# Rows of the heads' scratch arrays in DRAM: 4352 bytes apart in place of 4104

## The chip, the cores and the metric

The kernel runs on one core of a Trainium2 chip. The metric is the device time of one execution in microseconds (us); shorter is better. The kernel before takes 1936.97 us (median of three runs, 1929.43 to 1939.34).

A core has engines that run side by side, each with its own list of instructions in a fixed order: TensorE (PE, matmuls; PEld is its loading of weights), VectorE (DVE), ScalarE (ACT), GpSimd (POOL) and SyncE (SP). An instruction waits for the semaphores of what it needs, and everything behind it on its engine waits with it. SP issues all of this kernel's transfers; 16 DMA engines carry them out, a row of a tile as one packet.

## The reference

One layer of a decoder trunk on 1024 tokens, of width 1024, with 16 learned tokens in front. Two branches of four heads each (GLA and mLSTM) read the same normed input, are gated and merged; a gated MLP with a causal convolution follows.

```python
def mixer_block(h, w_in, b_in, ...):
    proj = h @ w_in + b_in
    (g_q, g_k, g_v, g_r, g_lr, m_q, m_k, m_v, m_o, m_i, m_f, gate_a, gate_b) = jnp.split(proj, splits, axis=-1)
    ...
    o_gla = from_chunks(head_rms(o_gla, gla_norm)) * jax.nn.silu(g_r)
    ...
    o_ml = from_chunks(head_rms(o_ml, ml_norm)) * jax.nn.sigmoid(m_o)
    y = jax.nn.sigmoid(gate_a) * (o_gla @ w_branch_gla) + jax.nn.sigmoid(gate_b) * (o_ml @ w_branch_ml)
    return y @ w_out

def reference(...):
    h = h + mixer_block(rms_norm(h, norm_mix), ...)
    h = h + conv_ffn(rms_norm(h, norm_ffn), ...)
    return rms_norm(h, norm_final)[:, N_META:, :]
```

## The kernel before

Activations lie with channels on the 128 partitions and tokens along the row. Each float32 factor is split into a high and a low part (xH, xL and so on), and a product is the sum of three matmuls. After the input has been normed (xH, xL), the work goes in stages:

- **Gates and values** (to about 510 us). Gates g_r, m_o, gate_a and part of gate_b, and the values of the heads s = 2 to 7, are computed as 2 by 2 block products with seven multiplications; this holds for the values of heads s = 2 and 3 too, before and after the change alike. The gates go to DRAM: `rdr` (16 channel blocks), `gsc["a"]` and `gsc["b"]` (8 blocks each). `gate_store` writes each pair of blocks in two transfers, goA (the first 514 of a row's 1026 numbers) and goB (the other 512).
- **Heads** (about 510 to 1015 us). Eight heads, s = 0 to 3 by `gla`, s = 4 to 7 by `mlstm`. While one head's side chain runs (decay, scores, states, outputs on DVE, ACT and PE), PE fills the time with projections for the next head, and in the last two heads with the first GLA branch products (`branch_gla`, which reads the heads' outputs back into xH and xL by `load_og`, L1369). A table of numbers, FILL, fixes where the side chain's steps stand between the projections; the result is a fixed order per engine.
- **End of a head**, `post`: the head's output, 256 channels as two blocks j = 0, 1, is scaled (L591), transposed (L603), multiplied with the gate r (L605, L614), split into oH (L616) and the rest, left in r (L617), and stored to `osc[g, "H"]` (L618) and `osc[g, "L"]` (L619): four transfers of 128 rows of 1026 numbers per head. The buffers are few: oH of j = 0 shares its buffer (`of`) with KT of the next head (L800 in gla, L913 in mlstm), oH of j = 1 (`oH`) with An of the next head (L711), and the two r buffers are loaded anew by `load_r` (L507) for the next head. So each of these writes waits for the store that reads the buffer.
- **Loads in the heads' stage.** SP issues in its fixed order. Behind an r load that waits for a store stand the loads of weights (L102), of MB and WB (rows for mlstm, L873 and L875), of v (L498, L499) and of xH and xL.
- **Branches and output** (about 1015 to 1210 us). The rest of the GLA branch products, then the mLSTM branch products (L1453), which read `osc["m"]` back as omH and omL, the gates from `gsc` (yg, sb) and the finished products from `ysc`; then the product with w_out (L1832), whose sums go to `hsc` (rows of 1024 numbers).
- **MLP** (about 1210 us to the end).

The arrays that the change touches are osc (four of 8 blocks: g and m, H and L), gsc (two of 8), rdr (16) and ysc (8). A block is 128 rows, one for each partition, and a row has NP = 1026 float32 numbers, 4104 bytes. All transfers of these arrays move rows of 4104 bytes, or in `gate_store` of 2056 and 2048 bytes.

Of the kernel before, what the change touches and what calls it, by code (L numbers as in the profile page):

```python
# [9 lines left out]
F32 = mybir.dt.float32  # L10
# [7 lines left out]
P = 128  # L18
# [4 lines left out]
NK = D // P  # L23
NP = SEQ + 2
# [21 lines left out]
def hybrid_kernel(ctx, tc, x, meta, norm_mix, w_in, b_in, gla_w_gate, gla_b_gate, gla_norm,  # L46
# [17 lines left out]
    dram = ctx.enter_context(tc.tile_pool(name="dram", bufs=1, space=DRAM))  # L64
# [360 lines left out]
                                pattern=[[1, P]], channel_multiplier=-1)  # L425


    osc = {(g, p): dram.tile([NK, P, NP], F32, name=f"osc{g}{p}") for g in "gm" for p in "HL"}
    gsc = {g: dram.tile([NK, P, NP], F32, name=f"gsc{g}") for g in "ab"}
    rdr = dram.tile([2 * NK, P, NP], F32, name="rdr")  # L430
    rsc = dram.tile([2, H, T], F32, name="rsc")

    heads = {}
# [654 lines left out]
    def gate_piece(q, p):  # L1088

        n, at = (W0, W1)[p], W0 * p  # L1090
        V, X, Y, Z = (psG.tile([P, 512], F32, name=f"g{b}{q}_{p}", tag=f"{b}{p}") for b in "VXYZ")
        if p == 0:
            gout[q] = (gp.tile([P, 2, NA], F32, name=f"goA{q}", tag="oA", bufs=2),
                       gp.tile([P, 2, 512], F32, name=f"goB{q}", tag="oB"))
        oA, oB = gout[q]
        u2 = g_u2[:, p, :n]
        g1, g2 = (oA[:, i, at:at + n] for i in range(2))
        e1, e2 = (oB[:, i, 256 * p:256 * p + 256] for i in range(2))
        h2 = slice(n - 256, n)
        gate_product(V, q, p, "A12", "B21", True, True)  # L1100
        gate_product(X, q, p, "A11", "B11", True, True)
        with hp(PRI_E):
            nc.scalar.activation(g1, V[:, :n], AF.Copy)
            first.append(nc.vector.tensor_tensor(g1, X[:, :n], g1, OP.add))
        yield
        gate_product(Y, q, p, "S1", "T1", True, True)
        gate_product(Z, q, p, "S3", "T3", True, True)
        yield
        gate_product(X, q, p, "S2", "T2", False, True)
        with hp(PRI_E):  # L1110
            nc.scalar.activation(u2, X[:, :n], AF.Copy)
            nc.vector.tensor_tensor(e2, Y[:, h2], u2[:, h2], OP.add)
            nc.vector.tensor_tensor(e2, Z[:, h2], e2, OP.add)
        yield
        gate_product(Y, q, p, "S4", "B22", False, True)
        gate_product(Z, q, p, "A22", "T4", False, True)
        with hp(PRI_E):
            nc.vector.tensor_tensor(e1, Y[:, h2], u2[:, h2], OP.add)  # L1118
            nc.vector.tensor_tensor(g2, Z[:, :n], u2, OP.add)
        func, c = GP[q][3:]  # L1120
        for i, e, g in ((1, e2, g2), (0, e1, g1)):
            for v in (e, g):
                nc.scalar.activation(v, v, func, bias=cc(c + i))  # L1123
        yield
# [136 lines left out]
    for q in range(len(GP)):  # L1261
        for p in range(2):
            g = gate_piece(q, p)
# [95 lines left out]
        while not ready():  # L1359
            advance()  # L1360

    ysc = dram.tile([NK, P, NP], F32, name="ysc")
    og = []

    def load_og():
# [369 lines left out]
    def piece(q, p):  # L1735

        n = (W0, W1)[p]
        V, X, Y, Z = (psF.tile([P, 512], F32, name=f"{b}{q}_{p}", tag=f"{b}{p}") for b in "VXYZ")
        if q not in us:
            us[q] = [r2.tile([P, T], F32, name=f"ug{q}", tag="Y5"), r2.tile([P, T], F32, name=f"uu{q}", tag="Y2")] \  # L1740
                if q % 2 == 0 else [r2.tile([P, T], F32, name=f"u{i}{q}", tag=f"O{p_}3b") for i, p_ in enumerate("HL")]
            us[q].append(spare["u2"])
        ug, uu, u2 = us[q]
        u2 = u2[:, p, :n]
        g1, g2 = (u[:, W0 * p:W0 * p + n] for u in (ug, uu))
        e1, e2 = (u[:, 514 + 256 * p:770 + 256 * p] for u in (ug, uu))
        h2 = slice(n - 256, n)
        product(V, q, p, "A12", "B21", True, True)
        product(X, q, p, "A11", "B11", True, True)
        with hp(PRI_E):  # L1750
            nc.scalar.activation(g1, V[:, :n], AF.Copy)
            nc.vector.tensor_tensor(g1, X[:, :n], g1, OP.add)
        yield
        product(Y, q, p, "S1", "T1", True, True)
        product(Z, q, p, "S3", "T3", True, True)
        yield
        product(X, q, p, "S2", "T2", False, True)
        with hp(PRI_E):
            nc.scalar.activation(u2, X[:, :n], AF.Copy)  # L1759
            nc.vector.tensor_tensor(e2, Y[:, h2], u2[:, h2], OP.add)  # L1760
            nc.vector.tensor_tensor(e2, Z[:, h2], e2, OP.add)
        yield
        product(Y, q, p, "S4", "B22", False, True)
        product(Z, q, p, "A22", "T4", False, True)
        with hp(PRI_E):
            nc.vector.tensor_tensor(e1, Y[:, h2], u2[:, h2], OP.add)
            nc.vector.tensor_tensor(g2, Z[:, :n], u2, OP.add)
        yield
# [144 lines left out]
    for q in range(NJ):  # L1913
        for p in range(2):
            g = piece(q, 1 - p if q == NJ - 1 else p)
# [289 lines left out]
```

## Time and profile before

| | |
|---|---|
| median of three runs | 1936.97 us |
| the profiled execution's own time | 1939.23 us |
| its span | 1937.5 us |
| PE busy | 1863.5 us (96%) |
| DVE busy | 1297.9 us (67%) |
| ACT busy | 930.3 us (48%) |
| DMA, share of 16 engines' span | 57.8% |
| moved by DMA | 322.99 MB, mean 167 GB/s |

The profile is of one execution. Its slices are 40 equal parts of the span; a digit is the busy share in tenths. The timeline has one row for each instruction or run of like instructions: start and length in us, engine, line, operation, what is written and read, and in brackets the idle time before it and what ended it. SPq stands for SP's queue; its rows are the issues of transfers, not the transfers themselves. PEclk is the share of full clock that TensorE was granted.

### The profile page before, as it was taken

Reading aid. Unit: us, or ns where it says so; the run is one execution under the profiler, and the core shown is the slowest. Engines: PE = TensorE matmul, PEld = TensorE weight load, DVE = VectorE, ACT = ScalarE, POOL = GpSimd, SP = SyncE. Lnnn points to the kernel's source line nnn. Section 1 sums busy time; section 2 is a strip of 40 time slices with the busy share of each in tenths; the row PEclk is TensorE's granted clock in tenths of the full one; section 3 lists DMA queues with packets and bytes.
Section 4 is the critical chain, followed back from the end, with each engine's and each line's share of the span. In section 5 each row is a group of like instructions: output and inputs, shape, how many; then the busy total and the mean of one; then the engine's idle time right before and its main releaser. Section 6 shows DMA issues by size and latency. Waiting matters only on the chain. (4 is left out here: it accounts for less than half of the span.)

```text
span 1937.5 us, 32927 instructions
## 1 busy us (share of the span) xinstructions
PE 1863.5 (96%) x13221; PEld 1774.6 (92%) x13221; DVE 1297.9 (67%) x1965; ACT 930.3 (48%) x1595; POOL 242.8 (13%) x218
## 2 busy tenths in 40 slices
PE   8999999999999999898799999999999999999997
PEld 6999999999989998787798999999999999988886
DVE  7654555577566556665541566698878889877867
ACT  5344444433456678655430223854434344446645
POOL 4200000000122112000000000013222232200000
PEclk9999999999999999989899999999999999999999
DMA  4343444444504466589899988433333454689986
GB/s 147 91 120 110 126 112 118 124 146 137 159 22 110 99 88 110 116 144 221 205 152 276 306 314 318 137 112 112 100 115 104 147 162 142 188 270 334 363 292 223
DMA packets 256166, 322.99 MB, mean 167 GB/s; under 512 B 14439, under 2 KB 196961, under 8 KB 254349
## 3 DMA queue, kind: packets, MB, share of 16 engines
q1 hardware_dynamic: 256013, 320.88, 57.8%
q8 instruction: 104, 1.70, 0.4%
q14 instruction: 49, 0.40, 0.1%
HBM read 232.01 MB, written 88.82 MB: 166 GB/s over the span
## 5 line engine op out<-in xcount | busy, mean ns | idle before, releaser
L1966 DVE TENSOR_TENSOR ringL<-f,ringH 128x1024 fp32r<-128x1024 f32 (+1 forms) x76 | 79.9, 1066 | 19.3 <-ACT ringH L1965 19.2
L1965 ACT ACTIVATE ringH<-f 128x1024 fp32r<-128x1024 f32 (+1 forms) x76 | 69.2, 928 | 33.7 <-DMA f<-in_ffn_w_down_dram 25.8
L1832 PE MATMUL po<-wH_wo,yH 128*128 128x256 f32 x256 | 73.7, 288 | 0.7 <-DVE sb L1548 0.7
L1832 PE MATMUL po<-wL_wo,yH 128*128 128x256 f32 x256 | 73.7, 288 | 0.0
L1832 PE MATMUL po<-wH_wo,yL 128*128 128x256 f32 x256 | 73.3, 286 | 0.0
L681 POOL TENSOR_TENSOR pk<-pk,kT 128x256 f32<-128x256 f32 (+1 forms) x40 | 51.3, 1305 | 123.6 <-ACT pk L679 112.8
L1781 DVE SCALAR_TENSOR_TENSOR cv<-u,fc,cv 128x1024 f32<-128x1024 f32 x44 | 65.9, 1500 | 0.4
L1709 POOL TENSOR_TENSOR SB<-SA,rg 128x512 f32<-128x512 f32 x20 | 27.9, 1397 | 232.3 <-issue 100.7
L1691 POOL TENSOR_TENSOR A<-u2raw,A 128x512 fp32r<-128x512 f32 x20 | 43.3, 2164 | 87.8 <-ACT A L1690 87.8
L1066 POOL TENSOR_TENSOR gA<-gu2raw,gA 128x512 fp32r<-128x512 f32 x14 | 18.0, 1287 | 280.5 <-ACT gA L1065 280.5
L1690 ACT ACTIVATE HA<-rg 128x1024 fp32r<-128x1024 f32 x16 | 17.0, 1060 | 72.6 <-PE Y L1732 62.2
L1832 PEld LDWEIGHTS po<-wH_wo,yH 128*128 128x128 f32 x256 | 50.0, 195 | 0.9 <-issue 0.9
L2004 ACT ACTIVATE aH<-f 128x768 fp32r<-128x768 f32 (+1 forms) x38 | 35.5, 933 | 30.5 <-PE dV L2029 20.1
L1832 PEld LDWEIGHTS po<-wH_wo,yL 128*128 128x128 f32 x256 | 50.1, 196 | 0.0
L1832 PEld LDWEIGHTS po<-wL_wo,yH 128*128 128x128 f32 x256 | 50.0, 195 | 0.0
L2005 DVE TENSOR_TENSOR aL<-f,aH 128x768 fp32r<-128x768 f32 (+1 forms) x38 | 40.6, 1067 | 13.9 <-ACT aH L2004 12.0
L1383 PE MATMUL bg<-xL,wH_bg 128*128 128x342 f32 x120 | 39.9, 333 | 10.3 <-DMA xL<-oscgL 10.3
L1759 ACT ACTIVATE u2raw<-X 128x258 f32<-128x258 f32 (+1 forms) x44 | 16.4, 373 | 65.7 <-PE X L1732 65.7
L1453 PE MATMUL bm<-omL,wH_bm 128*128 128x342 f32 x144 | 46.1, 320 | 1.5 <-DMA omL<-oscmL 1.5
L1123 ACT ACTIVATE goB<-goB,col 128x256 f32<-128x256 f32 x56 | 28.2, 504 | 37.2 <-DVE goB L1118 22.3
L1453 PE MATMUL bm<-omH,wL_bm 128*128 128x342 f32 x144 | 46.0, 320 | 0.0
L1453 PE MATMUL bm<-omH,wH_bm 128*128 128x342 f32 x144 | 46.0, 319 | 0.0
(777 smaller groups left out, 7860.7 us busy)
## 6 DMA issues: line engine op xcount, KB each, us to landing
f<-wts SPq DMA_DIRECT2D x38, 512.0 KB
vr<-in_w_in_dram SPq DMA_DIRECT2D x24, 512.0 KB
wsH<-in_ffn_w_down_dram SPq DMA_DIRECT2D x11, 1024.0 KB
wts<-wsL SPq DMA_DIRECT2D x11, 1024.0 KB
rg<-in_ffn_w_up_dram SPq DMA_DIRECT2D x22, 512.0 KB
ru<-in_ffn_w_up_dram SPq DMA_DIRECT2D x22, 512.0 KB
ad<-a SPq DMA_DIRECT2D x44, 256.0 KB
wr_wo<-in_w_out_dram SPq DMA_DIRECT2D x18, 512.0 KB
```

Source lines behind the costliest of these rows:

```text
L681: nc.gpsimd.tensor_tensor(e, e, k, OP.mult)
L1123: nc.scalar.activation(v, v, func, bias=cc(c + i))
L1383: nc.tensor.matmul(pts[i][:, :n], a[:, k, :], b[k][:, t0:t0 + n], start=(k == 0 and m == 0), stop=(k == NK - 1 and m == 2))
L1453: nc.tensor.matmul(pts[i][:, :n], a[:, k, :], b[k][:, t0:t0 + n], start=(k == 0 and j == 0), stop=(k == NK - 1 and j == 2))
L1691: eng.tensor_tensor(l, src, h.bitcast(F32), OP.subtract)
L1709: late.tensor_tensor(sb[:, 0:4], sa[:, 0:4], rg[:, 0:4], OP.subtract)
L1781: nc.vector.scalar_tensor_tensor(y, u[:, j:SEQ + j], fc[:, j, jj:jj + 1], y, OP.mult, OP.add)
L1832: nc.tensor.matmul(pt[:, :DV], a, b[:, k % 4, :], start=(k == 0 and i == 0), stop=(k == NK - 1 and i == len(terms) - 1))
L1965: nc.scalar.activation(h, raw, AF.Copy)
L1966: splits.append(nc.vector.tensor_tensor(l, raw, h.bitcast(F32), OP.subtract))
L2004: nc.scalar.activation(h, a[:, :n], AF.Copy)
L2005: nc.vector.tensor_tensor(l, a[:, :n], h.bitcast(F32), OP.subtract)
```

## The change

The four osc arrays, the two gsc arrays, rdr and ysc are allocated with rows of 1088 numbers (4352 bytes), and every use goes through a view of the first 1026 numbers of each row. The 62 numbers behind are neither written nor read. What is computed, the transfers, their sizes in bytes and the order of the instructions on each engine stay as they are. The distance between a head's H and L arrays goes from 1024 rows of 4104 bytes to 1024 rows of 4352 bytes.

```diff
-    osc = {(g, p): dram.tile([NK, P, NP], F32, name=f"osc{g}{p}") for g in "gm" for p in "HL"}
-    gsc = {g: dram.tile([NK, P, NP], F32, name=f"gsc{g}") for g in "ab"}
-    rdr = dram.tile([2 * NK, P, NP], F32, name="rdr")
+    osc = {(g, p): dram.tile([NK, P, 1088], F32, name=f"osc{g}{p}")[:, :, :NP] for g in "gm" for p in "HL"}
+    gsc = {g: dram.tile([NK, P, 1088], F32, name=f"gsc{g}")[:, :, :NP] for g in "ab"}
+    rdr = dram.tile([2 * NK, P, 1088], F32, name="rdr")[:, :, :NP]
...
-    ysc = dram.tile([NK, P, NP], F32, name="ysc")
+    ysc = dram.tile([NK, P, 1088], F32, name="ysc")[:, :, :NP]
```

## The prediction

> **What bounds the kernel now.** I read the page first, and in it the slices, since a mean over the span hides stages.
>
> ```profile
> PE   8999999999999999898799999999999999999997
> DMA  4343444444504466589899988433333454689986
> GB/s 147 91 120 110 126 112 118 124 146 137 159 22 110 99 88 110 116 144 221 205 152 276 306 314 318 137 112 112 100 115 104 147 162 142 188 270 334 363 292 223
> ```
>
> A slice is 48.4 us. TensorE is the bound nearly everywhere, so a change pays only where PE falls below 9: slices 16, 18 and 19 (775 to 823 us and 872 to 969 us), the stage of the heads. There the DMA row and the GB/s row disagree: slice 20 has its engines 9 tenths busy for 152 GB/s, slice 37 as busy for 363 GB/s. Something in the heads' stage makes transfers long without moving bytes. So I asked for windows around single transfers (columns: the stretch, its length, busy time of five engines, granted clock, DMA share, GB/s; a packet counts whole in the window where it starts, so a share can pass 1):
>
> ```profile
> 603.00:604.50 1.50, 1.50 (x11) 1.50 (x10) 1.50 (x4) 0.00 (x0) 0.00 (x0) 1.00 0.98 380
> 604.50:611.00 6.50, 6.50 (x47) 6.48 (x46) 6.25 (x9) 3.94 (x5) 2.87 (x2) 1.00 0.73 68
> 686.00:704.00 18.00, 18.00 (x130) 17.23 (x129) 9.99 (x11) 16.99 (x30) 3.98 (x5) 1.00 0.98 93
> 912.00:930.00 18.00, 9.53 (x40) 6.99 (x38) 11.05 (x18) 7.31 (x13) 0.00 (x0) 0.90 1.18 89
> 118.50:120.50 2.00, 2.00 (x19) 2.00 (x18) 1.44 (x4) 1.73 (x3) 0.00 (x0) 1.00 0.96 345
> 953.00:954.50 1.50, 1.50 (x12) 1.50 (x11) 1.20 (x5) 0.00 (x0) 0.12 (x1) 1.00 0.82 331
> 1198.00:1201.00 3.00, 3.00 (x27) 3.00 (x27) 0.93 (x3) 1.02 (x4) 0.00 (x0) 1.00 0.99 362
> 938.00:942.00 4.00, 4.00 (x17) 3.60 (x17) 0.71 (x4) 1.31 (x5) 0.00 (x0) 0.75 1.03 417
> ```
>
> The stores of the window at 1198 are SP's row
>
> ```profile
> 1197.46 1.19 SPq L1617 DMA_DIRECT2D hsc<-h  x2
> ```
>
> At 603 us the first of a head's four stores into osc (513 KB, 128 rows of 4104 bytes end to end) runs at 380 GB/s. When the second follows at once, the rate falls to 68 GB/s and stays there until both are drained; four in a row hold the queue near 90 GB/s for 18 us (686 and 912). Three controls stand below. At 118.5 us goA is stored into the same kind of array, rows 4104 bytes apart but only 2056 bytes of each: 345 GB/s. At 953 us ysc, whole rows, one store alone: 331 GB/s. At 1198 us two stores of hsc back to back, rows of 4096 bytes, 4096 apart: 362 GB/s for 3 us. And loads of 4104-byte rows run at 417 GB/s (938). So neither volume nor reading is slow; whole 4104-byte rows, laid end to end and written one store after another, are.
>
> What waits for them, in order of time (engine rows of the timeline; in brackets the idle time before the row and what ended it):
>
> ```profile
> 762.73 0.60 ACT L711 ACTIVATE An<-sct 128x512 f32<-128x512 f32 x1 [3.70 <-DMA oscgH<-oH]
> 824.37 1.29 DVE L913 TENSOR_TENSOR KT<-kt,tcol 128x512 f32<-128x512 f32 x2 [6.43 <-DMA oscgH<-oH]
> 848.64 0.20 DVE L897 COPY gp<-WB 128x8 f32<-128x8 f32 x1 [4.13 <-DMA WB<-rsc]
> 896.23 0.17 DVE L897 COPY gp<-WB 128x8 f32<-128x8 f32 x1 [3.93 <-DMA WB<-rsc]
> 917.94 1.29 DVE L913 TENSOR_TENSOR KT<-kt,tcol 128x512 f32<-128x512 f32 x2 [5.04 <-DMA oscmH<-oH]
> 1039.75 1.23 DVE L1497 TENSOR_TENSOR yg<-bg,yg 128x1026 f32<-128x1026 f32 x1 [22.75 <-DMA yg<-gsca]
> ```
>
> An and KT are written into the buffers that oH was stored from, so they wait until the store has read them. WB waits differently: SP issues in order, and its load of r ahead of WB waits for the store of the old r.
>
> ```profile
> SPq L507 <- DMA oscgL<-r: 103.4, 8, 16.4
> 908.01 0.32 SPq L618 DMA_DIRECT2D oscmH<-oH  x1
> 909.69 0.32 SPq L619 DMA_DIRECT2D oscmL<-r  x1
> 910.91 0.32 SPq L618 DMA_DIRECT2D oscmH<-oH  x1
> 912.17 0.32 SPq L619 DMA_DIRECT2D oscmL<-r  x1
> 912.54 0.45 SPq L1369 DMA_DIRECT2D xL<-oscgL  x1
> ```
>
> The first row is SP's wait list: 103.4 us in 8 times. The others are its issues: a load of xL right behind four stores. What reaches TensorE:
>
> ```profile
> 772.38 0.27 PE L790 MATMUL k0t<-ident,kh 128*16 128x128 f32 x1 [3.06 <-DVE kh L770]
> 805.55 0.33 PE L603 MATMUL ot<-ident,or 128*128 128x128 f32 x1 [1.89 <-ACT or L591]
> 825.12 2.08 PE L920 MATMUL msc<-qc,kc 128*128 128x128 f32 x8 [5.85 <-DVE KT L913]
> 855.64 0.33 PE L603 MATMUL ot<-ident,or 128*128 128x128 f32 x1 [1.19 <-ACT or L591]
> 900.41 1.53 PE L603 MATMUL ot<-ident,or 128*128 128x128 f32 x4 [3.11 <-ACT or L591]
> 918.69 0.70 PE L937 MATMUL u<-v,K 16*128 16x257 f32 x2 [3.63 <-DVE KT L913]
> 935.46 0.65 PE L1383 MATMUL bg<-xL,wH_bg 128*128 128x342 f32 x1 [10.29 <-DMA xL<-oscgL]
> 1041.12 0.39 PE L1453 MATMUL bg<-xH,wH_bg 128*128 128x342 f32 x1 [2.88 <-DVE yg L1497]
> 1055.82 0.43 PE L1453 MATMUL bm<-omL,wH_bm 128*128 128x342 f32 x1 [1.48 <-DMA omL<-oscmL]
> ```
>
> After such a gap the granted clock is 0.50 for a while (columns as above):
>
> ```profile
> 772.80:776.20 3.40, 3.40 (x16) 3.40 (x15) 3.34 (x3) 2.23 (x6) 0.00 (x0) 0.50 1.06 310
> 825.20:834.20 9.00, 9.00 (x24) 7.02 (x25) 5.58 (x10) 3.95 (x8) 0.00 (x0) 0.50 1.13 67
> 902.50:905.90 3.40, 3.40 (x15) 2.99 (x14) 1.26 (x3) 2.96 (x7) 0.00 (x0) 0.50 0.63 251
> 919.60:923.00 3.40, 3.40 (x9) 2.66 (x9) 3.40 (x5) 1.79 (x5) 0.00 (x0) 0.50 1.22 75
> 935.50:940.00 4.50, 4.50 (x14) 4.14 (x15) 0.16 (x1) 0.38 (x1) 0.00 (x0) 0.50 1.00 406
> 1042.50:1045.80 3.30, 3.30 (x13) 3.30 (x12) 2.36 (x2) 0.00 (x0) 0.00 (x0) 0.50 0.99 397
> ```
>
> **The change, part by part.** It adds and removes no instruction and moves none: the order on all five engines is the same, and every transfer keeps its 4104 (or 2056 and 2048) bytes per row. Only addresses change: a row begins 4352 bytes after the last, 17 times 256, so every row starts at a multiple of 256 from its array's start, and 248 unwritten bytes part it from the next.
>
> The unknown is the rate of whole-row stores at the new pitch, one behind another. Bounds by the nearest rows: 362 GB/s (hsc, separate aligned starts) and 93 GB/s (now); and below nothing, if lone row ends cost more than shared ones (a rival below). I take the fast end, since the new stores resemble the hsc pair in start and the goA store in not touching their neighbours, and both ran fast. A store of 525,312 bytes then takes 1.4 us at 362 to 380 GB/s.
>
> The loads of these rows gain nothing: 417 GB/s already. The stores of gsc, rdr and ysc gain nothing either where they come singly (345 and 331). So everything hangs on osc: eight heads with four stores each. Early heads (602 to 740 us) have their slow drains under a busy PE, so they gain nothing. From 760 us on, gap by gap:
>
> 772: ACT's 3.70 us on An goes; kh follows on ACT and DVE. 3.70 is more than PE's 3.06, so **3.1**. 825: DVE was ready for KT at 817.94 (824.37 less 6.43) and KT takes 1.29, so it ends at 819.2; PE arrives at 819.27 (825.12 less 5.85). The whole **5.9** goes. 918: likewise KT at 912.90 to 914.2, PE there at 915.06: **3.6**. 855 and 900: these chains run through gp, whose waits of 4.13 and 3.93 exceed PE's 1.19 and 3.11: **4.3**. 935: four stores and the load behind them are five transfers of 1.4 us, 7 us from 908.8, so xL lands near 917 even with 1 us for the issue; PE wants it at 925.17, or about 5 us earlier once 918 is mended, 920: **10.3**. 1041 and 1055: yg waits 22.75 us behind the last head's stores and stores of ysc; with those drained PE's 2.88 and 1.48 go: **4.4**. Sum of gaps: 31.6.
>
> Clock: the six stretches at 0.50 hold 3.4 + 9.0 + 3.4 + 3.4 + 4.5 + 3.3 = 27.0 us of matmuls; at full clock they take half: **13.5**. The 1.89 at 805 has no store wait in front and stays. Together 45.1 us.
>
> What is late next: with gaps closed, PE meets the ends of the heads' scalar chains sooner, as at 805, where 1.89 us cost another 3.4 us at half clock, 1.7 in loss. I leave two such places, 3.6 us each: 7 us given back. So 38 us from the profiled execution's own 1939.2 (span 1937.5 and 1.7 around it): **1901 us**. That execution lies 2.3 above the median of 1936.97 and at the slow end of three that differ by 9.9 us; I count from its own rows.
>
> **Against the trace: two rules.** The 417 GB/s of loads whose rows start at any multiple of 8 bytes is the row for the first. The Trainium skill, DMA: Bandwidth & Descriptors, section How a descriptor splits into AXI transactions, says that a read which does not start on 256 bytes fetches from the boundary below; for 4104 bytes I work out an estimate of 137 beats against 129, 6%. By that alone the sum would be zero, as the transfers that wait here are not 6% but four times too long. The rows at 686 and 912, four times below 362, are the ones for the second: the same page, section Latency and other measured facts, reports that padding a 4 MiB row pitch by 192 bytes left copies slow, and by 4 KiB made them fast. Its pitches are far larger than ours, yet it speaks against 248 bytes as a cure; by it the sum is again zero. The hsc pair, at a pitch of 4096 and fast, shows that a round pitch near this size is no harm here.
>
> **The rivals.** *Half a cure*: what costs is an incomplete line at a row's end. Today both ends of nearly every row are incomplete, later only the last 8 bytes. For it: hsc, without any, is fast. Against: goA has as many and is fast. A store's drain would halve: 18 us of drain become 9. The KT wait at 825 would end near 819, the xL load near 922; most gaps close, but WB, yg and a few us at 935 stay. I give it half to two thirds of 38, 19 to 25: about 1917.
>
> *No cure*: the slowness comes from the two arrays (H and L lie 1024 rows, 4.0 MiB now and 4.25 MiB later, apart) or from stores in a row as such. For it: the single stores at 603 and 953 are fast, and the slow ones are always H and L mixed. Against: the hsc pair. It gives the time of now, 1937. The two rules above belong here, with this chance.
>
> *Slower*: now the end of one row and the start of the next fall into one line and may be completed together; with a gap, 128 lone ends per store never are. Place: the drain behind L618 and L619. If a store took half as long again as now, 18 us becoming 27, KT in four heads (6.43, 5.04 and two smaller) would wait some 4 us more each and xL 9 more, less what the gaps before it already shift: about 20 us, 1957. It decides once four stores take longer than the 18 us of now. Against it: goA, whose row ends are lone when it is stored, at 345 GB/s.
>
> **How the numbers follow.** Full cure 0.70 (1890 to 1911: 45 us and a little of 805 at the best, 28 at the worst), half 0.13 (1911 to 1925), none 0.11 (1932 to 1941), slower 0.06 (1950 to 1965). The range 1890 to 1925 takes in the first two, 0.83, less a little at their edges. A measurement of this kernel tells about 0.5%, 9.7 us, from no change, so faster is under 1927: 0.70 + 0.13 = 0.83; same 0.11; slower 0.06.
>
> **What would show it.** Right: four osc stores drained within 7 us of the first, at over 300 GB/s; KT, An and gp without DMA waits; L507 on SP waiting for oscL a few us in place of 103.4; PE without the gap at 935, and clock 0.50 only near 772 or 805. The slices 17 to 20 should show lower DMA shares. Wrong: drains of 90 GB/s again (no cure), of some 180 (half), or gaps of the same length that now wait for DVE or ACT chains in place of DMA, which would mean that I missed what is late next.

## The result and the profile after

| | before | after |
|---|---|---|
| median | 1938.15 us (4 runs, 1929.43 to 1943.69) | 1885.66 us (4 runs, 1882.99 to 1888.39) |
| ratio | | 0.9733 (95%: 0.9693 to 0.9773) |
| profiled execution, own time | 1939.23 us | 1884.03 us |
| its span | 1937.5 us | 1882.3 us |
| PE busy | 1863.5 us (96%) | 1846.2 us (98%) |
| packets of the kernel's DMA queue (q1), share of 16 engines' span | 57.8% | 51.8% |

Faster, by 52.5 us between the medians and 55.2 between the profiled executions. The forecast was 1901 (1890 to 1925): the sign and the mechanism hold, and the gain is larger than the range allowed.

The slices of the page of after, each 47.1 us:

```profile
PE   7999999999999999999999999999999999999997
DMA  4334344345513143247758987433333545589986
GB/s 151 92 115 116 111 126 114 122 146 157 170 29 104 54 135 104 92 163 278 263 207 297 316 304 275 131 100 109 108 100 113 162 141 165 180 307 330 369 279 226
```

PE is at 9 in every slice but the first and the last. Counted from 0, as in the prediction, slice 17 (800 to 847 us) now has its DMA engines 4 tenths busy for 163 GB/s and slice 18 7 tenths for 278; before, slice 17 had them 8 tenths busy for 144 and slice 18 9 tenths for 221.

Windows around the stores into osc in after (columns as in the prediction):

```profile
602.50:604.00 1.50, 1.50 (x13) 1.48 (x12) 1.50 (x5) 0.91 (x1) 0.00 (x0) 1.00 0.98 386
673.50:681.00 7.50, 7.50 (x57) 7.50 (x55) 7.50 (x11) 4.16 (x5) 1.42 (x2) 1.00 0.82 305
886.00:892.00 6.00, 6.00 (x43) 5.33 (x42) 5.22 (x11) 1.14 (x2) 0.00 (x0) 1.00 1.03 372
```

The first store runs as before (386 against 380 GB/s). Four in a row, which were held near 90 GB/s, now move at 305 to 372. SP's timeline shows the same from the side of who waits. The rows are those of head 1, first of before, then of after; a load of r (L507) can only start once the store that reads its buffer (L619) has ended:

```profile
672.06 0.33 SPq L618 DMA_DIRECT2D oscgH<-oH  x1
...
686.83 0.32 SPq L507 DMA_DIRECT2D r<-rdr  x1
702.03 0.32 SPq L507 DMA_DIRECT2D r<-rdr  x1
```

```profile
673.01 0.33 SPq L618 DMA_DIRECT2D oscgH<-oH  x1
674.27 0.33 SPq L619 DMA_DIRECT2D oscgL<-r  x1
676.69 0.32 SPq L618 DMA_DIRECT2D oscgH<-oH  x1
678.00 0.32 SPq L619 DMA_DIRECT2D oscgL<-r  x1
678.42 0.40 SPq L507 DMA_DIRECT2D r<-rdr  x1
682.09 0.53 SPq L507 DMA_DIRECT2D r<-rdr  x1
```

From the head's first store to the second load of r it was 30.0 us; it is 9.1. SP's wait list of after says it for all heads:

```profile
SPq L507 <- DMA oscgL<-r: 18.6, 6, 6.2
SPq L507 <- DMA oscmL<-r: 5.9, 3, 2.3
```

Together these are 24.5 us; before, the two kinds took 103.4 and 31.9.

The DMA row does not show the whole of such a drain. In head 0 of before, L was stored at 603.36 and the load of r that waits for this store was issued at 616.49, yet in the last 4 us no packet starts (columns as above):

```profile
612.50:616.40 3.90, 3.90 (x27) 3.90 (x26) 3.90 (x5) 2.08 (x3) 3.29 (x3) 1.00 0.00 0
```

In after the two issues stand at 601.88 and 605.25. When a store has ended is therefore read from who waits for it. What DVE waits for on DMA between 755 and 1060 us, before and then after (us in total, times, longest):

```profile
DVE yg L1497 <- DMA yg<-gsca: 23.4, 2, 22.8
DVE KT L913 <- DMA oscmH<-oH: 10.2, 3, 5.0
DVE gp L897 <- DMA WB<-rsc: 9.0, 3, 4.1
DVE KT L913 <- DMA oscgH<-oH: 6.4, 1, 6.4
```

```profile
DVE wsL L1525 <- DMA wsp<-wspL: 7.5, 1, 7.5
```

All four are gone. What is left of PE's waits between 755 and 1250 us in after (every entry over 0.3 us):

```profile
PE ot L603 <- ACT or L591: 1.9, 1, 1.9
PE sct L710 <- DVE A L734: 1.6, 1, 1.6
PE htp L1643 <- ACT hn L1628: 1.6, 2, 0.8
PE Y L1732 <- DVE uu L1760: 1.1, 1, 1.1
PE htp L1643 <- ACT hT L1649: 0.8, 1, 0.8
PE po L1832 <- DVE sb L1548: 0.7, 1, 0.7
PE bg L1453 <- DVE bs L1387: 0.6, 1, 0.6
PE k0t L790 <- DVE kh L770: 0.4, 1, 0.4
```

No DMA is among them, and neither KT nor xL. The 1.9 is the wait that stood at 805 and now stands at 801. Stage by stage (the same stretches of before, then of after):

```profile
805.00:855.00 50.00, 43.05 (x220) 37.88 (x220) 29.74 (x73) 29.29 (x56) 2.11 (x5) 0.83 0.91 144
900.00:950.00 50.00, 35.45 (x175) 30.29 (x176) 21.59 (x40) 20.53 (x45) 0.00 (x0) 0.83 0.93 217
```

```profile
805.00:855.00 50.00, 50.00 (x311) 45.98 (x311) 38.03 (x81) 35.70 (x65) 2.11 (x4) 1.00 0.55 189
900.00:950.00 50.00, 50.00 (x302) 46.42 (x301) 29.96 (x70) 22.66 (x54) 1.79 (x1) 1.00 0.63 235
```

In 50 us PE now runs 302 to 311 matmuls where it ran 175 to 220. It has no gap there and a granted clock of 1.00 instead of 0.83.

### The profile page after: what moved, and what is told of

Same layout as the page of the kernel before. It is cut to its first block, busy times and chain, and to the rows that moved or that the text cites. A ratio compares the mean times of both kernels' runs of the same rounds, so it can differ in the third digit from the quotient of the medians.

```text
span 1882.3 us, 32927 instructions
## 1 busy us (share of the span) xinstructions
PE 1846.2 (98%) x13221; PEld 1760.5 (94%) x13221; DVE 1298.1 (69%) x1965; ACT 930.2 (49%) x1595; POOL 241.5 (13%) x218
## 3 DMA queue, kind: packets, MB, share of 16 engines
q1 hardware_dynamic: 256013, 320.88, 51.8%
## 4 chain that ended last, share of the span: by engine, by line
PE 82%; DVE 7%; ACT 4%; DMA 2%; issue 2%; POOL 1%; SPq 0%; DVEq 0%; POOLq 0%; ACTq 0%
PE pj L172 9%; PE Y L1732 6%; PE Z L1732 6%; PE X L1732 6%; PE bm L1453 5%; PE gX L1083 4%; PE gY L1083 4%; PE gZ L1083 3%; PE V L1732 3%; PE bg L1383 3%; PE po L1832 3%; PE dY L2029 2%; PE dZ L2029 2%; PE dX L2029 2%; PE pv L217 2%
## 5 line engine op out<-in xcount | busy, mean ns | idle before, releaser
L1690 ACT ACTIVATE HA<-rg 128x1024 fp32r<-128x1024 f32 x16 | 17.0, 1060 | 72.6 <-PE Y L1732 72.6
L2004 ACT ACTIVATE aH<-f 128x768 fp32r<-128x768 f32 (+1 forms) x38 | 35.5, 933 | 32.4 <-PE dV L2029 22.3
L1123 ACT ACTIVATE goB<-goB,col 128x256 f32<-128x256 f32 x56 | 28.2, 503 | 37.2 <-DVE goB L1118 22.3
L1118 DVE TENSOR_TENSOR goB<-gY,gu2raw 128x256 f32<-128x256 f32 x28 | 11.8, 421 | 49.5 <-PE gY L1083 49.5
```

## The experiments

All kernels keep the computation, the transfers and the order of instructions; only the addresses of scratch arrays differ. The arrays are allocated one behind another in the order of the program (gH, gL, mH, mL for osc), so one array's size is the distance between a head's H and L block. Sizes were set and addresses were not seen, so all distances below rest on this order. Each group ran on one chip beside the kernel before, whose median was 1933.04 (13 runs), 1932.82 (7) and 1934.14 (16).

### Which arrays

**osc_only** changes osc alone:

```diff
-    osc = {(g, p): dram.tile([NK, P, NP], F32, ...) for g in "gm" for p in "HL"}
+    osc = {(g, p): dram.tile([NK, P, 1088], F32, ...)[:, :, :NP] for g in "gm" for p in "HL"}
```

> Only the four osc arrays get rows 4352 bytes apart; gsc, rdr and ysc stay at 4104. If all of the gain comes from the heads' stores into osc (theory), the time is that of the changed kernel, 1886 us within 4. If the single stores of gsc, rdr and ysc count as well (rival), 5 to 15 us of the 52 are missing: 1891 to 1901.

**others_only** changes gsc, rdr and ysc, and leaves osc:

```diff
-    gsc = {g: dram.tile([NK, P, NP], F32, ...) for g in "ab"}
-    rdr = dram.tile([2 * NK, P, NP], F32, ...)
+    gsc = {g: dram.tile([NK, P, 1088], F32, ...)[:, :, :NP] for g in "ab"}
+    rdr = dram.tile([2 * NK, P, 1088], F32, ...)[:, :, :NP]
...
-    ysc = dram.tile([NK, P, NP], F32, ...)
+    ysc = dram.tile([NK, P, 1088], F32, ...)[:, :, :NP]
```

> gsc, rdr and ysc get rows 4352 bytes apart; osc stays at 4104. Theory (osc alone): the time of before, 1938 us within 5. Rival (the others count): 1923 to 1933.

osc_only took 1884.61 us, ratio 0.9745 (0.9730 to 0.9761); others_only 1932.95, ratio 0.9996 (0.9981 to 1.0011). PE's wait list of others_only still begins

```profile
PE bg L1383 <- DMA xL<-oscgL: 11.0, 1, 11.0
PE u L937 <- DVE KT L913: 6.0, 2, 5.3
PE msc L920 <- DVE KT L913: 6.0, 2, 4.1
PE ot L603 <- ACT or L591: 6.0, 2, 4.0
```

So the whole gain comes from osc, and padding the three other arrays does nothing for the time; the 1938 that was expected for it was an earlier median of before. In osc_only PE waits for yg no more, though gsc, from which yg is loaded, and ysc are as before: that load stood behind the osc stores. DVE still waits 12.8 us for yg there, where it waited 22.8; in after it does not. One thing in others_only is not explained: its two early heads drain in 8.9 and 22.3 us where before takes 13.1 and 30.0 (measured as in the table below), although osc is the same. With one trace of each kernel, differences of this size in the drains are not to be relied on, and no time came of them.

### Which heads

**osc_g** pads only the arrays of heads 0 to 3, **osc_m** only those of heads 4 to 7:

```diff
-    osc = {(g, p): dram.tile([NK, P, NP], F32, ...) for g in "gm" for p in "HL"}
+    osc = {(g, p): dram.tile([NK, P, 1088 if g == "g" else NP], F32, ...)[:, :, :NP] for g in "gm" for p in "HL"}
```

> Only the osc arrays of heads 0 to 3 get rows 4352 bytes apart. If the gain is the sum of the waits that I listed, each by the store it hangs on, this takes away 772 (3.1 and 1.7 of clock), 825 (5.9 and 4.5) and 855 (1.2): 16 us, so 1917 beside 1933 for before. Rival: the gaps hang together, and a gap closed early is paid again at the next slow store: under 8 us, over 1925.

(osc_m has `g == "m"` in that place.)

> Only the osc arrays of heads 4 to 7 get rows 4352 bytes apart. By the sum of waits it takes away 868 (0.6), 900 (3.1 and 1.7), 918 (3.6 and 1.7), 935 (10.3 and 2.3), 1041 and 1055 (4.4 and 1.7), and what lay behind 1060 us in the profile of before (the first product of the second norm, 3.1 of its 3.9 us, and its clock, about 2): 34 us, so 1899 beside 1933. With osc_g it should add up to the 48 of all four within 5. Rival: the two add up to less than 40 or more than 56.

osc_g took 1909.21 us, ratio 0.9890 (0.9864 to 0.9916), 23.6 less than before; osc_m 1903.58, ratio 0.9853 (0.9825 to 0.9882), 29.2 less. Together 52.8 against 48 for both halves at once: within the scatter, the two add up. The waits left on PE are those of the half that is not padded; osc_g first, osc_m second:

```profile
PE u L937 <- DVE KT L913: 5.2, 1, 5.2
PE bg L1383 <- DMA xL<-oscgL: 4.0, 1, 4.0
PE bm L1453 <- DMA omL<-oscmL: 3.0, 1, 3.0
```

```profile
PE msc L920 <- DVE KT L913: 6.0, 1, 6.0
PE ot L603 <- ACT or L591: 5.8, 2, 3.9
PE k0t L790 <- DVE kh L770: 3.1, 1, 3.1
```

The split differs from what was expected by 5 to 8 us each way. The load of xL at 935 reads a padded array in osc_g and PE still waits 4.0 us for it; in osc_m, where it is not padded, PE does not wait. What holds it are the stores of the mLSTM heads ahead of it in SP's queue. In osc_g this wait fell by 6.3 us, most of what osc_g gained beyond its forecast. The forecast of osc_m had counted some 5 us behind 1060 us that were not the stores' (see the base of the prediction below); without them it is 29 us, beside 29.2 measured.

### The gap between rows, the start of rows, or the distance of the arrays

The change alters three things at once: rows no longer touch, they start at multiples of 256 bytes, and the H and L arrays move apart, from 4 MiB + 8 KiB to 4 MiB + 256 KiB. The following eight take them apart. The old line of osc is the same in each diff and is left out.

**far_apart**: rows end to end as before, blocks and arrays as far apart as in the change.

```diff
+    osc = {(g, p): dram.tile([NK, P * 1088], F32, ...)[:, :P * NP].rearrange("k (p n) -> k p n", n=NP) for g in "gm" for p in "HL"}
```

> osc keeps rows end to end, 4104 bytes apart, but each block of 128 rows starts where it does in the changed kernel, so H and L lie the same 4.25 MiB apart as there. If the slowness comes from the distance of the two arrays (rival), 1886 us. If it comes from the rows themselves, their starts or their touching ends (theory), 1938 us within 5 and drains of four stores near 90 GB/s.

**pitch4360**: a gap of 256 bytes, but rows that start at multiples of 8 bytes only.

```diff
+    osc = {(g, p): dram.tile([NK, P, 1090], F32, ...)[:, :, :NP] for g in "gm" for p in "HL"}
```

> osc rows 4360 bytes apart: a gap of 256 bytes between rows as in the changed kernel, but rows start at any multiple of 8 bytes, as before. If touching row ends cost (theory A), 1886 us within 4. If starts off a boundary cost (theory B), 1938 us within 8, since 7 of 8 rows start off every 64-byte boundary.

pitch4360 took 1885.45 us, ratio 0.9749 (0.9731 to 0.9766): the whole gain, so aligned starts are not needed. far_apart was expected at the time of before and took 1895.75, ratio 0.9814 (0.9791 to 0.9837): most of the gain with rows that touch. The theory that touching rows alone are at fault fell here, and the rival that was called *No cure* in the prediction, the distance between the arrays, came back.

**arrays_apart**: rows and blocks end to end, only the arrays as far apart as in the change.

```diff
+    osc = {(g, p): dram.tile([NK * P * 1088], F32, ...)[:NK * P * NP].rearrange("(k p n) -> k p n", p=P, n=NP) for g in "gm" for p in "HL"}
```

> osc rows end to end, 4104 bytes apart, blocks of 128 rows end to end as before (525,312 bytes), but the arrays H and L as far apart as in the changed kernel (4.25 MiB in place of 4 MiB and 8 KiB). far_apart had both distances and gained 37 of 48 us. If the distance of H and L is what counts, 1896 us; if the distance of block 0 and block 1 is, 1933; if both count in part, between them.

**pitch4112**: a gap of 8 bytes.

```diff
+    osc = {(g, p): dram.tile([NK, P, 1028], F32, ...)[:, :, :NP] for g in "gm" for p in "HL"}
```

> osc rows 4112 bytes apart: 8 bytes between rows, so most rows still share a stretch of 64 bytes with the next; blocks lie 526,336 bytes and H and L 4 MiB and 16 KiB apart, near the distances of before. If rows in one stretch of 64 bytes cost, or the near distances do, 1925 to 1938; if only ends that meet byte to byte cost, 1885 within 5.

arrays_apart took 1902.25 us, ratio 0.9849 (0.9826 to 0.9873); pitch4112 1893.16, ratio 0.9801 (0.9769 to 0.9832). pitch4112 lies 8 us above what was expected of a gap alone. Its gap of 8 bytes brings 40 us, but it also moves the arrays to 4 MiB + 16 KiB apart. Four more separate the two:

**apart8**: end to end, the arrays 8 MiB + 8 KiB apart. **apart16k** is the same line with 1028 * 1024 numbers, 4 MiB + 16 KiB apart.

```diff
+    osc = {(g, p): dram.tile([2099200], F32, ...)[:NK * P * NP].rearrange("(k p n) -> k p n", p=P, n=NP) for g in "gm" for p in "HL"}
```

> osc rows end to end as before; each array takes 8 MiB and 8 KiB, so that H and L lie 8 KiB past a multiple of 4 MiB apart, as before, but are no longer neighbours. If the distance by its remainder is what arrays_apart changed (theory D), 1933 us within 5. If any larger distance helps (rival), 1895 to 1907.

> osc rows end to end, arrays 4 MiB and 16 KiB each: the distance of H and L of pitch4112 without its 8 bytes between rows. If the gap made pitch4112's 40 us (theory A), 1925 to 1937; if its 8 KiB of distance did (theory D), 1890 to 1905.

**padded_apart8**: rows 4352 bytes apart as in the change, the arrays 8 MiB + 8 KiB apart.

```diff
+    osc = {(g, p): dram.tile([2099200], F32, ...)[:NK * P * 1088].rearrange("(k p n) -> k p n", p=P, n=1088)[:, :, :NP] for g in "gm" for p in "HL"}
```

> osc rows 4352 bytes apart, arrays of 8 MiB and 8 KiB. If the gap between rows is enough by itself (theory A), 1885 us within 4, whatever the distance. If the distance by its remainder counts beside it (theory D), 1895 to 1925.

**pitch4160**: a gap of 56 bytes, rows that start at multiples of 64.

```diff
+    osc = {(g, p): dram.tile([NK, P, 1040], F32, ...)[:, :, :NP] for g in "gm" for p in "HL"}
```

> osc rows 4160 bytes apart: every row starts on 64 bytes and none shares 64 bytes with the next; H and L 4 MiB and 64 KiB apart. If a shared stretch of 64 bytes is what pitch4112 (1893) had left, 1885 us within 4; if it is the distance, 1890 to 1897.

All of them together. "Head 0" is the time from the issue of its first L store to the load of r behind it, "head 1" from its first store to the second load of r (the two stretches shown for before and after above), both from SP's timeline of the profiled execution.

| | gap, bytes | H to L beyond a multiple of 4 MiB | median us | ratio (95%) | head 0, us | head 1, us |
|---|---|---|---|---|---|---|
| before | 0 | 8 KiB | 1932.8 to 1934.1 | | 13.1 | 30.0 |
| apart8 | 0 | 8 KiB | 1930.74 | 0.9986 (0.9956 to 1.0016) | 13.0 | 27.9 |
| apart16k | 0 | 16 KiB | 1919.42 | 0.9918 (0.9889 to 0.9947) | 12.0 | 28.5 |
| arrays_apart | 0 | 256 KiB | 1902.25 | 0.9849 (0.9826 to 0.9873) | 7.4 | 16.9 |
| far_apart | 0 (blocks apart) | 256 KiB | 1895.75 | 0.9814 (0.9791 to 0.9837) | 7.3 | 11.8 |
| pitch4112 | 8 | 16 KiB | 1893.16 | 0.9801 (0.9769 to 0.9832) | 3.4 | 9.1 |
| pitch4160 | 56 | 64 KiB | 1886.76 | 0.9752 (0.9716 to 0.9787) | 3.4 | 9.1 |
| padded_apart8 | 248 | 8 KiB | 1888.86 | 0.9754 (0.9712 to 0.9797) | 3.1 | 9.1 |
| pitch4360 | 256 | 264 KiB | 1885.45 | 0.9749 (0.9731 to 0.9766) | 2.9 | 9.1 |
| after | 248 | 256 KiB | 1885.66 | 0.9733 (0.9693 to 0.9773) | 3.4 | 9.1 |

What lies behind the last column: the same 10 us of head 1, from 3 us after its first store, in apart8, arrays_apart, far_apart, pitch4112 and after:

```profile
676.50:686.50 10.00, 10.00 (x72) 10.00 (x72) 10.00 (x14) 5.45 (x6) 2.47 (x3) 1.00 1.15 80
676.80:686.80 10.00, 10.00 (x73) 10.00 (x71) 10.00 (x14) 5.45 (x6) 2.49 (x3) 1.00 1.16 128
676.00:686.00 10.00, 10.00 (x73) 10.00 (x72) 10.00 (x15) 5.45 (x6) 2.33 (x3) 1.00 1.03 225
678.00:688.00 10.00, 10.00 (x73) 10.00 (x72) 10.00 (x14) 5.44 (x6) 2.52 (x3) 1.00 0.84 264
676.00:686.00 10.00, 10.00 (x72) 10.00 (x71) 10.00 (x14) 5.46 (x6) 2.48 (x3) 1.00 0.80 261
```

With rows that touch the queue moves 80 GB/s at the old remainder of 8 KiB, 128 with the arrays 256 KiB past 4 MiB apart, and 225 with the blocks apart as well; with a gap of 8 or 248 bytes it moves 264 or 261. Three readings follow.

First, with touching rows the distance decides. Its size does not: at 8 MiB + 8 KiB (apart8) nothing is gained that is clear of the scatter, at 4 MiB + 256 KiB 31 us (arrays_apart). far_apart, with the blocks apart too, gains 37 us; the intervals of the two just overlap, so the distance between blocks probably counts as well. Second, with a gap the distance no longer matters much: padded_apart8 gains 45.3 us at the old remainder and osc_only 48.4 at 256 KiB, while padded_apart8 and apart8, at the same distance, differ by 42 us (1930.74 to 1888.86). Third, 8 bytes are most of the gap's worth: apart16k and pitch4112 have the same distance between H and L and differ by 26 us, each counted from its own chip's before as 14.7 and 39.7 us gained, 25 between them. So apart16k fits neither of its two forecasts; the gap and the 8 KiB of distance share pitch4112's 40 us. In these runs slow drains need both, rows that touch and an unlucky distance, and the change removed both; the gap alone would have brought 45 us (1934.14 to 1888.86), the distance alone 31 to 37.

osc_only, pitch4360, pitch4160 and the change itself lie within 2.2 us of each other; no version was found that is faster than the change.

## Why the prediction was right in its mechanism, and where it failed

**The mechanism held**, point by point. Four osc stores drain at 305 to 372 GB/s, as was taken from hsc and goA. An, KT and gp wait for no DMA. L507's waits fell from 103.4 to 18.6 us for oscgL; the 10.29 at 935 is gone; the only gap behind 750 us that still costs clock in the heads' stage is the one that stood at 805. That gsc, rdr and ysc gain nothing was right (others_only, 0.9996).

**Gaps and clock: 45.1 us in the sum, 48.2 measured.** The gaps of the sum, 31.6 us, shrink to 0.4 (k0t). A way to check the sum without trusting single rows is to compare the start of the same group in both kernels. The mLSTM branch products, first and last start in us at the end of the times (their ns are shortest, median and longest), before and then after:

```profile
L1453 PE MATMUL bm<-omH,wH_bm x144: 313/319/328, 1054.0 to 1145.4; 128*128 128x342 f32 x144
```

```profile
L1453 PE MATMUL bm<-omH,wH_bm x144: 315/319/328, 1008.9 to 1098.2; 128*128 128x342 f32 x144
```

After leads by 45.1 at the first and by 47.2 at the last. That the first equals the sum is chance: 1.48 us of the sum fall between the two, at 1055, and before the first of the gaps after was not level but 0.95 behind (head 1's first store, 672.06 and 673.01 above). So this stretch gained 48.2, 3.1 more than the sum. Two waits that the sum had left out are 1.7 of it: PE waits for S at 785 (1.3 us before, 0.2 after) and for KT at 868 (0.6 before, none after). The rest was not traced to single rows.

**What is late next: the first step that failed.** It took 7 us off for two new places like 805, 3.6 each. There is none: the waits of PE on the heads' DVE and ACT chains that the list above still has stood there before too, the 1.9 at 805 and 1.5 us where after has 1.6 (sct). The prediction gave these chains a price without a row that showed one being late. That they had slack hidden behind the DMA waits would explain it; the slack was not measured. Counting 45.1 from 1939.23 gives 1894, within the range.

**The base: the second step that failed.** The prediction counted from the profiled execution's own 1939.2, "from its own rows". The three groups of experiments gave before medians of 1932.8 to 1934.1 in 36 runs, 5.1 to 6.4 us lower. Take off the 7 us, the 3.1 and these 5.1 to 6.4, and 1901 becomes 1884.5 to 1885.8, beside the 1885.66 measured. The fast end of the range, 1890, allowed 45 us and a little of 805 from the high base, and neither a longer sum nor a lower base.

**The rest, to 55.2, does not come from the osc stores.** After's lead grows by 8 us more behind 1146, where no osc store is near. Of these, 5.3 are one place in before: the transposes htp that start at 1226.44 in before start at 1173.89 in after, a lead of 52.5. PE's wait list of before (755 to 1250 us) has

```profile
PE htp L1643 <- ACT hn L1628: 3.9, 1, 3.9
```

The timeline of DVE has the work ahead of it, and a window the clock behind it:

```profile
1205.22 1.23 DVE L1525 TENSOR_TENSOR wsL<-wsH 128x1024 f32<-128x1024 f32 x1 [3.33 <-DMA wsH<-in_ffn_w_down_dram]
```

```profile
1211.20:1216.20 5.00, 4.97 (x27) 4.95 (x28) 1.80 (x3) 3.76 (x12) 1.10 (x2) 0.50 0.86 309
```

A load of MLP weights came late by 3.33 us; PE lost 3.9, and some 2.5 more in the 5 us at half clock behind it (after has 1.6 us of such waits itself). Most of what is left of the 8 us comes between 1700 and 1800 us, where PE waits 3.2 us for DVE's u in before and 1.6 in after. In others_only, which gains nothing, the wait list and the window read

```profile
PE htp L1643 <- ACT hn L1628: 0.5, 1, 0.5
```

```profile
1209.60:1214.60 5.00, 5.00 (x45) 4.98 (x46) 2.32 (x6) 4.09 (x14) 1.04 (x2) 1.00 0.95 318
```

and the load is not waited for. apart8, which gains nothing either, waits 4.2 there, and padded_apart8, which gains all, 3.2; in these two the same row of DVE waits for a store of hsc. So this wait does not go with the osc drains. In size, 5.3 us, it accounts for the high base. That other executions of before are without it was not shown, since one was profiled.

**The reason given for the fast end was partly wrong.** The new stores were likened to hsc "in start": pitch4360 has unaligned starts and is as fast. They were likened to goA "in not touching their neighbours": that, in these runs, was the part that counts.

**The rivals.** *Half a cure* by incomplete lines at a row's end falls: all pitches with a gap of 56 bytes or more leave such ends, and all lie within 4.3 us of each other (1884.61 to 1888.86). *Slower* falls with it. *No cure* through the distance was half right: distance is a cause, as the runs with touching rows show, but the change moves the arrays too, by an amount that helps, and its gap helps at any distance tried. The two rules that were weighed do not explain the slowness. pitch4360's rows start at multiples of 8 bytes, as before, and it has the whole gain. A pad of 248 bytes cures at this pitch. The Trainium skill, DMA: Bandwidth & Descriptors, section Latency and other measured facts, tells of a pad of 192 bytes that did not, at a pitch of 4 MiB; no run here has such a pitch. The estimate of 137 beats that the prediction worked out from the Trainium skill (same page, section How a descriptor splits into AXI transactions) is one too high: a row of 4104 bytes that starts at a multiple of 8 takes 136 at most, 5% more than 129. Nothing hangs on it.

**What stays open** is why touching rows and the distance meet in this way. The stores of H and L follow each other by 1.3 us, faster than they drain. That a line shared by two rows is written twice, and that the two arrays then fall on the same part of the memory, is a guess. Lines of 64 bytes do not fit it well: in pitch4112 three of four rows still share such a stretch with the next, and its two early heads drain as fast as with any wider gap (3.4 and 9.1 us). Open too is whether it matters where touching rows meet. All touching rows of osc were 4104 bytes long; hsc's rows touch as well, at multiples of 4096 bytes, and ran at 362 GB/s, but in one array. No run separates the two.

## What to carry to other kernels

Where the DMA row of the slices reads 9 and the GB/s row is low, look for back-to-back stores of whole rows that touch (of 4104 bytes here), and try a gap: 8 bytes brought most of it, 56 bytes all. Test it on the one array that is written in bursts before padding the others, and judge by the waits of what is queued behind the stores, since the DMA row does not show a drain to its end. When a sum of gaps is made from one execution, compare its total with the median over several, and put a price on what is late next only where a row shows a chain that is late.

## What the runs showed of the hardware

- The rate of stores depends on things that no instruction shows: with the same stores of 525,312 bytes, the queue moved 80 GB/s (apart8), 128 (arrays_apart) or 225 (far_apart) with touching rows, by how far arrays and blocks lie apart, and 261 to 264 with a gap between rows (after, pitch4112).
- A store can end well after its last packet has started: in before, no packet starts from 612.50 to 616.40 us, and what waits for the store goes on at 616.49.
- The remainder of that distance counted, not its size: 8 KiB past 4 MiB and past 8 MiB were equally slow (1932.8 to 1934.1 and 1930.74 us), 16 KiB gained 15 us, 256 KiB 31 us.
- 8 bytes between rows brought 25 us at one distance, and with a gap of 56 bytes or more, whether rows start at a multiple of 256, of 64 or of 8 bytes made no difference that these runs can tell (1885.66, 1886.76, 1885.45 us).
- A half clock comes and goes without a change in the order. The window of 641 to 647 us in after,

```profile
641.00:647.00 6.00, 6.00 (x17) 4.14 (x16) 2.81 (x5) 4.71 (x7) 0.00 (x0) 0.50 0.02 5
```

ran at 0.50, though PE had waited for nothing since 600 us; the same stretch ran at 1.00 in before and in osc_only, and at 0.72 in others_only. It is why after, 2.2 us ahead of before in front of it (u of L815 starts at 638.92 and 641.16), is 0.95 behind at 672.
